# A hand-written order for the experts' stage, weight pieces split whole, and two weight streams for experts with up to 64 tokens

## The chip, the cores and the metric

The kernel runs on one NeuronCore of one Trainium2 chip. The metric is the device time of one execution in microseconds (us), as the median of several executions. The profile is one further execution, recorded by the hardware profiler.

## What is computed

A two-layer decoder trunk on 256 tokens of width 1024, everything in fp32. Each layer runs two groups of attention heads on one input projection, adds their output projection to the residual, and then a feed-forward part: layer 0 a dense SwiGLU of width 2816, layer 1 a router that sends every token to the best two of eight SwiGLU experts of width 3584. The change is about the last part:

```python
def swiglu(h, w_gate, w_up, w_down):
    return (jax.nn.silu(h @ w_gate) * (h @ w_up)) @ w_down

def moe_swiglu(h, router_w, w_gate, w_up, w_down):
    logits = (hf @ router_w).astype(jnp.float32)
    top_logit, top_e = lax.top_k(logits, TOP_K)
    gate = jax.nn.softmax(top_logit, axis=-1)
...
        return swiglu(hf[tok], w_gate[e], w_up[e], w_down[e])
...
    out = jnp.zeros((N, D), jnp.float32).at[row_tok].add(y.reshape(rows, D).astype(jnp.float32) * row_gate[:, None])
```

The router of the reference, on the reference's inputs, gives the eight experts 63, 57, 40, 75, 39, 90, 68 and 80 of the 512 token places. So experts 0, 1, 2 and 4 have at most 64 tokens, the other four have more, and none has over 128.

## The kernel before

**Pieces.** All large weights come from HBM as pieces of 1 MB, [128, 2048] fp32, in the order in which they are used (`Weights.load`, L64 to L73, one DMA each on SP's queue). TensorE multiplies in fp32r, which keeps fewer bits than fp32, so each weight is split into two parts whose sum is exact: ACT copies the piece to fp32r (`whi`, L94), and DVE subtracts that copy from the piece (`wlo`, L95). The data are split in the same way, and a product is three matmul streams (`product3`, L366 to L368): data hi by weight hi, data lo by weight hi, data hi by weight lo. Before, a piece is split in two halves of 1024 columns, and there are five buffers for `whi` and five for `wlo` (N_PART). The pieces themselves lie in four buffers (N_RAW), in the experts' stage also in eight more that attention has left (SPARE), which makes a ring of twelve.

**The experts' stage** (`moe`, from L782). After the router, `gather(e)` puts an expert's tokens into 128 slots: a one-hot matrix `so` picks them out of `h` (32 matmuls `ga`, L830), and ACT and DVE split them (`xe`). The width of 3584 is worked in 7 chunks of 512, so there are 8 x 7 = 56 steps (`seq`). A step uses six pieces: two of gate, two of up, and two of down for the chunk of the step before. Its matmuls, each 128 x 512 in the moving data: 24 `eg` (gate), then 4 `eT` that turn the product of the step before (`turn`, split by ACT into `eth` and by DVE into `etl`), 24 `eu` (up), and 24 `ey` (down). ACT takes Silu of `eg` (`esg`, L906), DVE multiplies with `eu` (`ehc`, L908). At an expert's end `weigh` scales both halves of `ey` with the gates (`yhl`, L304 on ACT, L305 on DVE), and four `scatter` steps (two matmuls and one DVE addition into `acc` each) put the slots back at their tokens, one per step. The next expert is gathered in chunk 3, all at once. `beyond` (behind `tc.If` at L974) would work on slots 128 and up, and is jumped over.

**What sets the order.** The Tile framework's scheduler orders the instructions of each engine from the program and its dependences. Each engine then runs its own list strictly in that order and waits on semaphores.

Of the kernel before, what the change touches and what calls it, by code (L numbers as in the profile page):

```python
# [49 lines left out]
N_RAW, N_PART, SPARE = 4, 5, 8  # L50


class Weights:
    """Weight tiles: loaded in the order of the list, fp32 in, an exact sum of two fp32r parts out."""

    def __init__(self, nc, specs, plain, raw_pool, part_pool, n_raw, n_part):
# [4 lines left out]
        self.spare = {}  # L61
        self.loaded = self.used = 0
# [17 lines left out]
    def take(self):  # L80
# [6 lines left out]
        out = []  # L87
        step = max(1, 1024 // w // 2 * 2)
        for k in range(0, nk, step):
            m = min(step, nk - k)  # L90
            src = raw[:, k:k + m, :].rearrange("p k w -> p (k w)")
            hi = self.part_pool.tile([128, 1024], F32R, name="whi", tag="whi", bufs=self.n_part)
            lo = self.part_pool.tile([128, 1024], F32R, name="wlo", tag="wlo", bufs=self.n_part)
            self.nc.scalar.activation(hi[:, :m * w], src, AF.Copy)  # L94
            self.nc.vector.tensor_tensor(out=lo[:, :m * w], in0=src, in1=hi[:, :m * w].bitcast(F32), op=ALU.subtract)  # L95
            out += [(hi[:, i * w:(i + 1) * w], lo[:, i * w:(i + 1) * w]) for i in range(m)]
        return out
# [3 lines left out]
def trunk_kernel(ctx: ExitStack, tc: tile.TileContext, T: dict, out: bass.AP):  # L101
# [26 lines left out]
    # ---------------------------------------------------------------- weights  # L128
# [52 lines left out]
    # the experts' pieces also go where attention has finished  # L181
# [3 lines left out]
    # -------------------------------------------------------------- constants  # L185
# [64 lines left out]
    # ones, and ones where the row is before the column: exact in bf16  # L250
# [5 lines left out]
    # distance bias, negated, and the mask, as rows over distance + 255  # L256
# [525 lines left out]
    def moe(l, mpool, ht):  # L782
# [137 lines left out]
        def down(e, c, th, tl):  # L920
# [14 lines left out]
            if c == 1:  # L935
                state["place"] = place(e)
# [196 lines left out]
```

## Time and profile before

| | |
|---|---|
| median of 3 runs | 1551.79 us (1550.57 to 1552.54) |
| span of the profiled execution | 1555.6 us (no other time of its own is given; 3.8 us above the median) |
| PE busy | 1527.9 us (98%), 7502 matmuls |
| DVE busy | 1235.4 us (79%) |
| ACT busy | 1026.8 us (66%) |
| POOL busy | 7.8 us (1%) |
| weight pieces of the experts | 336 of 1 MB, 352 of the 434 MB that SP's queue moves |
| experts' stage, first `eg` to the end | 540.8 to 1555.6 us |

PE is TensorE's matmul stream; a matmul's record overlaps the next one's, so the distance between two starts is what a matmul costs. "PEclk" is the granted clock of TensorE as a share of 2.4 GHz. PE has something to do nearly all the time, so the first question at every place is what one step costs on PE, and the second how far behind the next engine is.

### The profile page before, as it was taken

To read this page: it belongs to the slowest core of one execution; us is meant where nothing else is said; L and a number is where in the kernel's file an instruction comes from. 1 tells how busy PE (TensorE), PEld (TensorE's weight loads), DVE (VectorE), ACT (ScalarE), POOL (GpSimd) and SP (SyncE) were. 2 spreads that over 40 slices of the span, in tenths; PEclk is the share of its full clock that TensorE was granted. 3 is DMA by queue.
4 is the path that set the end of the run, shared out by engine and by line. 5 is a ranking of instruction groups with operands and counts; after the bars stand their busy time and mean duration, and the time that the engine had idled before them with its cause. 6 is when DMAs were issued, how large, how long until landed. Compare 5 with 4: busy or idle time off the path is not lost.

```text
span 1555.6 us, 20636 instructions
## 1 busy us (share of the span) xinstructions
PE 1527.9 (98%) x7502; PEld 1234.2 (79%) x7502; DVE 1235.4 (79%) x1771; ACT 1026.8 (66%) x1389; POOL 7.8 (1%) x17
## 2 busy tenths in 40 slices
PE   7999999999999999999999999999999999999997
PEld 6767888888777888888888878887887887887885
DVE  5567755555766798998998888988888889888886
ACT  5445644445545587887787777767777776767774
POOL 2000000000000000000000000000000000000000
PEclk9999999999999999999999999999999999999999
DMA  8812455557626499999999989999999999999980
GB/s 263 292 55 82 157 178 177 200 189 234 229 96 217 167 357 331 379 357 329 361 363 333 363 320 336 344 356 342 326 370 352 327 358 346 329 352 365 353 323 29
DMA packets 200907, 436.94 MB, mean 281 GB/s; under 512 B 9448, under 2 KB 26080, under 8 KB 200800
## 3 DMA queue, kind: packets, MB, share of 16 engines
q1 hardware_dynamic: 198160, 434.63, 79.2%
q8 instruction: 61, 1.00, 0.3%
q10 hardware_dynamic: 2176, 0.52, 0.2%
q0 software_dynamic: 464, 0.40, 0.1%
q14 instruction: 46, 0.38, 0.1%
HBM read 433.92 MB, written 1.08 MB: 280 GB/s over the span
## 4 chain that ended last, share of the span: by engine, by line
PE 95%; DMA 2%; DVE 2%; ACT 1%; issue 1%; SPq 0%; ACTq 0%; DVEq 0%
PE eu L368 7%; PE eg L368 7%; PE eu L367 6%; PE eu L366 6%; PE eg L367 6%; PE eg L366 6%; PE ey L366 6%; PE ey L367 6%; PE ey L368 6%; PE pj L368 3%; PE pj L366 3%; PE pj L367 3%; PE y L368 2%; PE y L367 2%; PE y L366 2%; PE o L502 2%
## 5 line engine op out<-in xcount | busy, mean ns | idle before, releaser
L95 DVE TENSOR_TENSOR wlo<-raw,whi 128x1024 fp32r<-128x1024 f32 (+1 forms) x802 | 946.1, 1215 | 158.9 <-ACT whi L94 147.9
L94 ACT ACTIVATE whi<-raw 128x1024 fp32r<-128x1024 f32 (+1 forms) x802 | 807.0, 1051 | 188.7 <-PE y L367 45.2
L368 PE MATMUL eg<-wlo,xe 128*128 128x512 f32 x448 | 177.4, 396 | 1.5 <-DVE wlo L95 1.5
L368 PE MATMUL eu<-wlo,xe 128*128 128x512 f32 x448 | 178.6, 399 | 0.0
L366 PE MATMUL ey<-whi,eth 128*128 128x512 f32 x448 | 177.5, 397 | 0.7 <-ACT eth L301 0.7
L366 PE MATMUL eg<-whi,xe 128*128 128x512 f32 x448 | 176.8, 395 | 0.7 <-ACT xe L304 0.3
L366 PE MATMUL eu<-whi,xe 128*128 128x512 f32 x448 | 177.4, 396 | 0.0
L367 PE MATMUL ey<-whi,etl 128*128 128x512 f32 x448 | 176.8, 395 | 0.0
L367 PE MATMUL eg<-whi,xe 128*128 128x512 f32 x448 | 175.9, 393 | 0.0
L367 PE MATMUL eu<-whi,xe 128*128 128x512 f32 x448 | 175.2, 391 | 0.0
L368 PE MATMUL ey<-wlo,eth 128*128 128x512 f32 x448 | 165.7, 399 | 0.0
L368 PEld LDWEIGHTS eu<-wlo,xe 128*128 128x128 f32 x448 | 84.1, 188 | 23.9 <-DVE wlo L95 6.9
L368 PEld LDWEIGHTS eg<-wlo,xe 128*128 128x128 f32 x448 | 84.2, 188 | 22.4 <-DVE wlo L95 4.6
L366 PEld LDWEIGHTS ey<-whi,eth 128*128 128x128 f32 x448 | 84.3, 188 | 20.7 <-ACT eth L301 1.1
L367 PEld LDWEIGHTS ey<-whi,etl 128*128 128x128 f32 x448 | 84.5, 189 | 20.2 <-DVE etl L302 0.4
L366 PEld LDWEIGHTS eg<-whi,xe 128*128 128x128 f32 x448 | 84.2, 188 | 20.3 <-ACT whi L94 2.6
L367 PEld LDWEIGHTS eg<-whi,xe 128*128 128x128 f32 x448 | 84.1, 188 | 17.8
L367 PEld LDWEIGHTS eu<-whi,xe 128*128 128x128 f32 x448 | 84.2, 188 | 17.1
L366 PEld LDWEIGHTS eu<-whi,xe 128*128 128x128 f32 x448 | 84.2, 188 | 15.8
L368 PEld LDWEIGHTS ey<-wlo,eth 128*128 128x128 f32 x448 | 82.5, 188 | 17.4
L301 ACT ACTIVATE eth<-eT 128x512 fp32r<-128x512 f32 x56 | 33.1, 592 | 88.7 <-PE ey L368 75.0
L366 PE MATMUL pj<-whi,uhi 128*128 128x512 f32 (+1 forms) x192 | 76.3, 399 | 0.8 <-ACT qv L411 0.8
(299 smaller groups left out, 1970.5 us busy)
## 6 DMA issues: line engine op xcount, KB each, us to landing
raw<-in_exp_w_gate_dram SPq DMA_DIRECT2D x112, 1024.0 KB, 7.0
raw<-in_exp_w_up_dram SPq DMA_DIRECT2D x112, 1024.0 KB, 7.0
raw<-in_exp_w_down_dram SPq DMA_DIRECT2D x112, 1024.0 KB, 6.8
raw<-in_w_in_dram SPq DMA_DIRECT2D x20, 1024.0 KB, 6.0
raw<-in_ffn_w_gate_dram SPq DMA_DIRECT2D x10, 1024.0 KB, 5.1
raw<-in_ffn_w_up_dram SPq DMA_DIRECT2D x10, 1024.0 KB, 5.2
raw<-in_ffn_w_down_dram SPq DMA_DIRECT2D x10, 1024.0 KB, 5.1
raw<-in_cmp_w_dram SPq DMA_DIRECT2D x8, 1024.0 KB, 6.2
```

What stands on the lines that cost most here:

```text
L94: self.nc.scalar.activation(hi[:, :m * w], src, AF.Copy)
L95: self.nc.vector.tensor_tensor(out=lo[:, :m * w], in0=src, in1=hi[:, :m * w].bitcast(F32), op=ALU.subtract)
L301: act.activation(hi, src, AF.Copy)
L366: pe.matmul(dst, xh, wh, start=first, stop=False)
L367: pe.matmul(dst, xl, wh, start=False, stop=False)
L368: pe.matmul(dst, xh, wl, start=False, stop=last)
L502: pe.matmul(o[:, hd * HD:(hd + 1) * HD], pt[:, c:c + 128], vpj[:, j, vc:vc + HD], start=(j == 0), stop=(j == nj - 1))
```

## The change

Four things change.

1. **Split whole.** `split()` makes one ACT and one DVE instruction of 2048 columns per piece; N_PART is three whole pieces (six halves' worth) and N_RAW three, so the ring has eleven pieces in the experts' stage and three elsewhere. This holds for attention and the dense feed-forward too.
2. **Order.** The experts' steps stand under `tc.manual_schedule()`: the program's order is each engine's order. `ahead(1)` splits one piece, three ahead of the one in use, after each product. The next expert's work is spread: slots in chunk 2, half of the gather in chunks 3 and 4, `rl` in chunk 5. `eT` comes at the end of a step.
3. **Two streams.** For an expert with at most 64 tokens (`few`), slots 64 to 127 hold the same tokens again (`own`). POOL copies the hi part of slots 0 to 63 and the lo part of slots 0 to 63 side by side (`mixed`: `xm` per expert, `htm` per step). A matmul with that as its weights gives hi and lo data at once, so up and down need two streams, 16 matmuls a step in place of 24. The sum of the two halves of the slots comes from `both` in the turn, and in the end from the scatter. Gate keeps three streams.
4. **Choice at run time.** The count of the expert is loaded into a register of PE (`value_load`, once per expert), and `by_number` puts an If with both forms around each up piece (2), the turn (1) and each down piece (2): 5 per step, 280 in all. The POOL copies run in both cases.

```diff
-N_RAW, N_PART, SPARE = 4, 5, 8
+N_RAW, N_PART, SPARE = 3, 3, 8
...
+        hi = self.part_pool.tile([128, 2048], F32R, name="whi", tag="whi", bufs=self.n_part)
+        lo = self.part_pool.tile([128, 2048], F32R, name="wlo", tag="wlo", bufs=self.n_part)
+        self.nc.scalar.activation(hi[:, :nk * w], src, AF.Copy)
+        self.nc.vector.tensor_tensor(out=lo[:, :nk * w], in0=src, in1=hi[:, :nk * w].bitcast(F32), op=ALU.subtract)
...
+    def ahead(self, n, loads):
+
+        for _ in range(n):
+            if self.used < len(self.specs):
+                self.ready.append(self.split())
+                self.load(self.used + loads)
...
+        def slots(e):
+
+            own = mpool.tile([128, 128], F32, name="own", tag="own")
+            dve.scalar_tensor_tensor(out=own, in0=again, scalar=few[:, e:e + 1], in1=slot, op0=ALU.mult, op1=ALU.add)
...
+            held[e] += rl, pe.value_load(number[0:1, e:e + 1], min_val=0, max_val=S)
...
+        def by_number(e, many, few):
+
+            with tc.If(held[e][3] > 64) as cond:
+                many()
+            with cond.Else():
+                few()
+
+        def mixed(src, name, n):
+
+            dst = mpool.tile([128, n, 128], F32R, name=name)
+            pool.tensor_copy(dst.rearrange("p k (i t) -> p i k t", i=2), src[:, :, :, 0:64])
+            return dst
...
+            def few():
+                for k, (wh, wl) in enumerate(w, k0):
+                    pe.matmul(b, mix[:, k, :], wh, start=(k == 0), stop=False)
+                    pe.matmul(b, mix[:, k, :], wl, start=False, stop=(k == last))
...
+                for f in range(4):
+                    pe.matmul(b[:, f * 128:(f + 1) * 128], hc[:, f * 128:(f + 1) * 128], both, start=True, stop=True)
...
+        with tc.manual_schedule():
+            prev = None
+            ws.ahead(N_PART, deep)
+            for step in seq + [None]:
+                if step is not None:
+                    e, c = step
+                    _, x, rl, _ = held[e]
+                    if c == 0:
+                        state["xm"] = mixed(x, "xm", KD)
+                    b = mm_bank("eg")
+                    for half in range(2):
+                        product(e, x, b, half * 4, ws.take(), None, KD - 1)
+                        if half:
+                            sg = mpool.tile([128, 512], F32, name="esg", tag="esg")
+                            act.activation(sg, b, AF.Silu, scale=rl)
+                        ws.ahead(1, deep)
+                    b = mm_bank("eu")
+                    for half in range(2):
+                        product(e, x, b, half * 4, ws.take(), state["xm"], KD - 1)
+                        if not half:
+                            ws.ahead(1, deep)
+                    hc = mpool.tile([128, 512], F32, name="ehc", tag="ehc")
+                    dve.scalar_tensor_tensor(out=hc, in0=b, scalar=rl, in1=sg, op0=ALU.mult, op1=ALU.mult)
+                    ws.ahead(1, deep)
+                if prev is not None:
+                    pe_, pc, hts = prev
+                    if pc == 0:
+                        state["y"] = [acc_bank("ey") for _ in range(2)]
+                    down(pe_, pc, 0, ws.take(), hts)
+                    ws.ahead(1, deep)
+                    down(pe_, pc, 2, ws.take(), hts)
+                    if pc == len(MOE_CHUNKS) - 1:
+                        out_of(pe_)
+                if step is not None:
+                    prev = e, c, turn(e, hc)
+                    ws.ahead(1 if (e, c) != seq[0] else 0, deep)
+                    if c == 1:
+                        state["place"] = place(e)
+                    if e + 1 < NE:
+                        if c == 2:
+                            slots(e + 1)
+                        if c in (3, 4):
+                            gather(e + 1, (c - 3) * 4)
+                        if c == 5:
+                            rstd_of(e + 1)
+                for _ in range(1 if step is not None else len(left)):
+                    if left:
+                        scatter(*left.pop(0))
```

Three places of the order, each before and after. First PE at the turn of a step: before, `eT` lies between `eg` and `eu`.

```order
2370 L367 MATMUL eg<-whi,xe 128x512
2371 L368 MATMUL eg<-wlo,xe 128x512
2372 L366 MATMUL eg<-whi,xe 128x512
2373 L367 MATMUL eg<-whi,xe 128x512
2374 L368 MATMUL eg<-wlo,xe 128x512
2375 L914 MATMUL eT<-cc,ehc 128x128 x4
2376 L366 MATMUL eu<-whi,xe 128x512
2377 L367 MATMUL eu<-whi,xe 128x512
2378 L368 MATMUL eu<-wlo,xe 128x512
```

After, at the end of a step, with the two forms of the last down piece and of the turn (L372 to L374 are now the three streams, L989 and L990 the two of `few`):

```order
2326 L374 MATMUL ey<-wlo,eth 128x512
2327 L928 UNCONDITIONAL_BRANCH
2328 L989 MATMUL ey<-whi,htm 128x512
2329 L990 MATMUL ey<-wlo,htm 128x512
2330 L989 MATMUL ey<-whi,htm 128x512
2331 L990 MATMUL ey<-wlo,htm 128x512
2332 L989 MATMUL ey<-whi,htm 128x512
2333 L990 MATMUL ey<-wlo,htm 128x512
2334 L989 MATMUL ey<-whi,htm 128x512
2335 L990 MATMUL ey<-wlo,htm 128x512
2336 L928 UNCONDITIONAL_BRANCH
2337 L928 COMPARE_AND_BRANCH
```

`eT` has moved behind the down product, and of every such block PE runs one of the two forms and jumps over the other.

Second DVE over a step, before (the multiplication `ehc`, the splits, `acc` of a scatter, `etl`):

```order
877 L908 SCALAR_TENSOR_TENSOR ehc<-eu,rl,esg 128x512
878 L95 TENSOR_TENSOR wlo<-raw,whi 128x1024 x4
879 L890 TENSOR_TENSOR acc_4841<-acc_4841,scat 128x512
880 L95 TENSOR_TENSOR wlo<-raw,whi 128x1024 x4
881 L302 TENSOR_TENSOR etl<-eT,eth 128x512
882 L95 TENSOR_TENSOR wlo<-raw,whi 128x1024 x4
883 L908 SCALAR_TENSOR_TENSOR ehc<-eu,rl,esg 128x512
```

And after (L92 is the split, L308 writes the lo half of `eth`):

```order
801 L1027 SCALAR_TENSOR_TENSOR ehc<-eu,rl,esg 128x512
802 L928 UNCONDITIONAL_BRANCH x2
803 L92 TENSOR_TENSOR wlo<-raw,whi 128x2048 x2
804 L308 TENSOR_TENSOR eth<-eT,eth 128x512
805 L92 TENSOR_TENSOR wlo<-raw,whi 128x2048 x2
806 L928 UNCONDITIONAL_BRANCH
807 L92 TENSOR_TENSOR wlo<-raw,whi 128x2048
808 L928 UNCONDITIONAL_BRANCH x2
809 L92 TENSOR_TENSOR wlo<-raw,whi 128x2048
810 L1027 SCALAR_TENSOR_TENSOR ehc<-eu,rl,esg 128x512
```

Twelve halves became six whole splits between two `ehc`, and the five Ifs of a step leave a branch instruction each in DVE's list, as in ACT's, SP's and POOL's.

Third POOL, which had no row between the start and the stage's end, and now has two kinds of copy:

```order
33 L936 COPY htm<-eth 128x2x4x64
34 L936 COPY xm<-xe 128x2x8x64
35 L928 UNCONDITIONAL_BRANCH x5
36 L936 COPY htm<-eth 128x2x4x64
37 L928 UNCONDITIONAL_BRANCH x5
38 L936 COPY htm<-eth 128x2x4x64
```

One copy of 512 elements per partition lies in every step, and one of 1024 at an expert's start.

## Rows read from the trace of the kernel before

**Rows 1.** The page: busy time of the engines.

```profile
PE 1527.9 (98%) x7502; PEld 1234.2 (79%) x7502; DVE 1235.4 (79%) x1771; ACT 1026.8 (66%) x1389; POOL 7.8 (1%) x17
```

**Rows 2.** The chain of waits from 530 us: start, us, what.

```profile
591.13 0.44 PE eT L914 x4
608.11 0.44 PE eT L914 x4
...
707.28 3.57 PE ga L830 x32
...
832.77 3.57 PE ga L830 x32
...
960.30 2.01 PE ga L830 x18
...
1087.67 2.01 PE ga L830 x18
```

**Rows 3.** PE's own instructions in a timeline: start, us, what.

```profile
904.42 0.39 PE L366 MATMUL eg<-whi,xe 128*128 128x512 f32 x1
...
904.65 0.40 PE L367 MATMUL eg<-whi,xe 128*128 128x512 f32 x1
```

**Rows 4.** DVE by form: busy us, mean ns, idle before.

```profile
L95 DVE TENSOR_TENSOR wlo<-raw,whi 128x1024 fp32r<-128x1024 f32 x794 | 940.3, 1220 | 156.8 <-ACT whi L94 145.8 <-PE pj L368 1.1 <-PE pj L367 0.4
L908 DVE SCALAR_TENSOR_TENSOR ehc<-eu,rl,esg 128x512 f32<-128x512 f32 x56 | 41.9, 749 | 18.0 <-PE eu L368 18.0
L302 DVE TENSOR_TENSOR etl<-eT,eth 128x512 fp32r<-128x512 f32 x56 | 38.5, 687 | 10.3 <-ACT eth L301 10.3
L305 DVE SCALAR_TENSOR_TENSOR xe<-ga,gv,xe 128x128 fp32r<-128x128 f32 x64 | 20.6, 346 | 10.4 <-ACT xe L304 10.2
L890 DVE TENSOR_TENSOR acc<-acc,scat 128x512 f32<-128x512 f32 x28 | 19.1, 683 | 4.5 <-PE scat L889 4.4
...
L305 DVE SCALAR_TENSOR_TENSOR yhl<-ey,gs,yhl 128x512 fp32r<-128x512 f32 x16 | 11.5, 746 | 8.4 <-ACT yhl L304 8.4
...
L95 DVE TENSOR_TENSOR wlo<-raw,whi 128x560 fp32r<-128x560 f32 x8 | 5.9, 736 | 2.1 <-ACT whi L94 2.1
```

**Rows 5.** DVE's timeline: splits without a wait between them.

```profile
555.27 3.49 DVE L95 TENSOR_TENSOR wlo<-raw,whi 128x1024 fp32r<-128x1024 f32 x3
```

**Rows 6.** ACT by form.

```profile
L94 ACT ACTIVATE whi<-raw 128x1024 fp32r<-128x1024 f32 x794 | 801.9, 1055 | 180.7 <-PE y L367 43.6 <-PE fu L367 32.7 <-PE eg L367 24.7
...
L94 ACT ACTIVATE whi<-raw 128x560 fp32r<-128x560 f32 x8 | 5.3, 673 | 8.0 <-PE pj L367 6.4 <-PE y L367 1.7
```

**Rows 7.** 20 us windows: PE, PEld, DVE, ACT, POOL, PEclk, DMA share, GB/s.

```profile
640.00:660.00 20.00, 20.00 (x93) 16.43 (x92) 18.38 (x18) 16.12 (x18) 0.00 (x0) 1.00 1.03 387
...
860.00:880.00 20.00, 20.00 (x91) 16.40 (x90) 18.22 (x18) 16.02 (x17) 0.00 (x0) 1.00 1.02 365
920.00:940.00 20.00, 19.60 (x85) 14.74 (x84) 18.30 (x19) 14.76 (x17) 0.00 (x0) 1.00 0.91 336
```

**Rows 8.** The page: DMA issues, us to landing.

```profile
raw<-in_cmp_w_dram SPq DMA_DIRECT2D x8, 1024.0 KB, 6.2
```

**Rows 9.** The If over `beyond` and its flag: min/median/max ns.

```profile
L974 PEldq COMPARE_BRANCH  x1: 4622/4622/4622, 1548.2 to 1548.2; - x1
L974 DVEq COMPARE_BRANCH  x1: 72/72/72, 1549.0 to 1549.0; - x1
...
L876 PEldq TENSOR_LOAD <-flag x1: 484/484/484, 1547.6 to 1547.6; - x1
```

**Rows 10.** PE's sequencer at a wait, and weight loads during it.

```profile
L559 PEldq EVENT_SEMAPHORE  x2: 1432/2636/3839, 48.7 to 396.3; - x2
...
400.45 0.59 PEld L559 LDWEIGHTS hid<-raw,xp 128*32 128x32 f32 x24 [0.35 <-issue]
```

**Rows 11.** 4 us windows around PE's pauses, columns as in group 7.

```profile
48.00:52.00 4.00, 2.31 (x12) 1.42 (x12) 4.00 (x22) 1.29 (x3) 0.00 (x0) 1.00 1.10 348
52.00:56.00 4.00, 4.00 (x41) 2.48 (x42) 3.86 (x17) 0.00 (x0) 0.00 (x0) 0.57 0.78 217
```

More of the change, by code (lines that the diff above doesn't have):

```diff
@@ L61, in __init__ @@
         self.spare = {}
+        self.ready = []
         self.loaded = self.used = 0
@@ L816, in moe @@
                                  op0=ALU.add, op1=ALU.mult)
+        cb = tr_bank("count")
+        for t in range(NT):
+            pe.matmul(cb[:, 0:NE], ones, sel[:, t, :], start=(t == 0), stop=(t == NT - 1))
+        few = mpool.tile([128, NE], F32, name="few")
+        dve.tensor_scalar(out=few, in0=cb[:, 0:NE], scalar1=64.0, scalar2=None, op0=ALU.is_le)
+        number = mpool.tile([128, NE], I32, name="number")
+        dve.tensor_copy(number, cb[:, 0:NE])
+        most = mpool.tile([128, 1], F32, name="most")
@@ new lines, in gather, with rstd_of @@
+        def gather(e, k):
+            so, x = held[e][:2]
+            b = tr_bank("ga")
+            for j in range(4):
+                for t in range(NT):
+                    pe.matmul(b[:, j * 128:(j + 1) * 128], h[t][:, (k + j) * 128:(k + j + 1) * 128], so[:, t, :],
+                              start=(t == 0), stop=(t == NT - 1))
+            for j in range(4):
+                split_psum(x[:, 0, k + j, :], x[:, 1, k + j, :], b[:, j * 128:(j + 1) * 128], gain(R_FN, l, k + j))
+        def rstd_of(e):
+            so = held[e][0]
@@ L867, in place @@
             return st, gs
-        cb = tr_bank("count")
-        for t in range(NT):
-            pe.matmul(cb[:, 0:NE], ones, sel[:, t, :], start=(t == 0), stop=(t == NT - 1))
-        most = mpool.tile([128, 1], F32, name="most")
-        dve.tensor_reduce(out=most, in_=cb[:, 0:NE], axis=AX.X, op=ALU.max)
         flag = mpool.tile([128, 1], I32, name="flag")
@@ L944, in moe @@
-        prev = None
-        left = []
-        parts_of = []
-        def between():
-            if prev is not None:
-                parts_of[:] = turn(prev[2])
-        for i, (e, c) in enumerate(seq):
-            if c == 3 and e + 1 < NE:
-                gather(e + 1)
-            hc = gate_up(e, c, between)
-            if prev is not None:
-                down(*prev[:2], *parts_of)
-            for _ in range(PER if c else 0):
-                if left:
-                    scatter(*left.pop(0))
-            prev = (e, c, hc)
@@ L962, in moe @@
-        between()
-        down(*prev[:2], *parts_of)
-        for e, n, t, st, yhl in left:
-            scatter(e, n, t, st, yhl)
+        def by_number(e, many, few):
[7 more added lines that the diff above has]
+            return dst
@@ new lines, in down, with steps, many, few @@
+        def down(e, c, k0, w, hts):
+            ht, htm = hts
+            y = state["y"]
+            ends = c == len(MOE_CHUNKS) - 1
+            def steps():
+                for i, (wh, wl) in enumerate(w):
+                    for n in range(2):
+                        f = slice(n * 512, (n + 1) * 512)
+                        yield y[n], k0 + i, wh[:, f], wl[:, f]
+            def many():
+                for o, k, wh, wl in steps():
+                    product3(o, ht[:, 0, k, :], ht[:, 1, k, :], wh, wl, c == 0 and k == 0, ends and k == 3)
+            def few():
+                for o, k, wh, wl in steps():
+                    pe.matmul(o, htm[:, k, :], wh, start=(c == 0 and k == 0), stop=False)
+                    pe.matmul(o, htm[:, k, :], wl, start=False, stop=(ends and k == 3))
+            by_number(e, many, few)
```

114 lines of the change are left out of this document (44 added, 70 removed).

## Prediction

> **What bounds the kernel now.** I read the busy times first: PE has work for 98% of the span, DVE for 79%, ACT for 66%, POOL for nothing [rows 1]. Then the chain of waits, for the period of a step: two turns of quiet steps start 16.98 us apart [rows 2], and matmuls start 0.23 us apart [rows 3], so 72 of them and the turn are the step, and PE's own work is what a step costs. From the gather of one expert to the next it is 125.5 us, later 127.5 and 127.4 [rows 2]; in the windows PE is full (20.00 of 20) except once per expert at its end, where it shows 19.60 and the period is 1.9 us longer [rows 7]: ACT holds the next splits behind `yhl`, which waits for the last `ey`. DVE has 16 to 18 us of work in such a 20 us window and the DMA engines a share of 0.91 to 1.03 [rows 7]. So the reader is to see a stage that PE sets, with two other resources close behind. A cut of PE's work gains only as far as the next one.
>
> **The two streams.** A few-step has 16 matmuls less: on PE 16.98 - 16 x 0.23 = 13.3 us. DVE keeps all of its work, so I add that up. A split of 2048 columns isn't in the trace. Columns cost (1220 - 736) / 464 = 1.043 ns each [rows 4]; three splits in a run take 3.49 us [rows 5], so one follows the other by (3.49 - 1.22) / 2 = 1.135, and 1024 more columns add 1.07: 2.20 us per whole split in a run. Bounds are 2.20 and 2.29 (one alone, 1.22 + 1.07); I take the run, since DVE now works without a pause. Per expert: 42 x 2.20 = 92.4, `ehc` 7 x 0.749 = 5.2, `etl` 7 x 0.687 = 4.8, `xe` 8 x 0.346 = 2.8, `acc` 4 x 0.683 = 2.7, `yhl` 2 x 0.746 = 1.5 [rows 4], and some 1.2 for slots, `rl` and gates (small ones, each under an `xe`). That is 110.6 us, or 15.8 a step: **DVE becomes the bound of the few-steps**, and 2.5 of the 3.7 us that PE gives up are lost to it. To it come waits within DVE's fixed list. Before, `ehc` waited 18.0, `etl` 10.3 and `xe` 10.4 us over eight experts [rows 4], together 4.8 per expert; the hand order puts two splits ahead of each, so I take 3 (bounds 0 and 4.8).
>
> **The POOL copies.** They are new, and nothing in the trace shows POOL and DVE at work together. By the nearest row of that size a copy of 512 columns is 0.69 us (`etl`). PE needs `htm` only after the next step's 24 gate and 16 up matmuls (9 us) and `xm` after 24 (5.5 us), so PE doesn't wait. What the copy costs DVE lies between nothing and its whole 0.69 us in each of 7 steps, 4.8 per expert; I take half, 2.4, as nothing shows which end is nearer. The Trainium skill has a rule that speaks against this part: "SBUF — State Buffer", section "Who interferes with whom", says that a DVE instruction with two SBUF inputs, as the split is, and a GpSimd instruction that reads SBUF exclude each other for the whole instruction. No row here can test it; by it the upper end holds, and that is a rival below.
>
> A few-expert is then 110.6 + 3 + 2.4 = 116.0 us. Experts 0, 1 and 2 took 125.5 each and expert 4 took 127.4: **gain 3 x 9.5 + 11.4 = 39.9 us.**
>
> **The four other experts.** PE's work stays. The hand order removes the hold at the expert's end (1.9 us), but a scatter now stands in PE's list where `yhl` is barely ready (about 1 us), and one where the bank of `etl` is (about 1 us). I take 0, bounds -1.9 and +2 per expert. Three whole parts are enough: a split takes ACT 1.055 + 1024 x (1055 - 673) / 464 = 1.90 us [rows 6] and DVE 2.29, 4.2 in a row and some 0.2 of signals, against 5.5 for the two pieces that PE works on meanwhile.
>
> **The Ifs.** 280 on PE, half of them with a taken jump over 12 pairs of instructions, half over 8. A compare and branch takes 72 ns on DVE and 4622 on PE, for one jump over all of `beyond` [rows 9]. The trace has no short jump on PE. Its sequencer runs ahead: it was held 3.84 us at a wait, and the weight loads behind it paused for 0.35 us only [rows 10], so what it loses at one If is covered by queued work unless it is over 3 us; in the few-steps another 3 us a step of slack come on top. I take nothing for PE (the other end is the slower rival). The load of the count is one per expert, 0.48 us [rows 9], covered likewise. On DVE five branch instructions a step could cost up to 5 x 0.072 us in the 28 few-steps, 10 us; they have nothing to compare, and I take 1.
>
> **DMA.** A few-step still needs six pieces, 6.29 MB, now in 16.6 us: 380 GB/s. The queue showed 387 at a share of 1.03 in its best window and 365 at 1.02 [rows 7], so at 365 it brings 5.78 pieces a step, and the ring drains by 0.22 a step, or 5 pieces over the 21 few-steps of experts 0 to 2; of eleven about eight are ahead. Expert 3 fills it again. I take no cost; if the lead goes, DMA is late next.
>
> **Start, end, attention.** At the start of the stage fewer pieces are loaded ahead (eleven buffers, not twelve), the first split is a whole piece (+1.9), and the router has some ten small instructions more while the gather keeps PE busy: 2 us. At the end the last splits are whole pieces: 1.5. In both attention layers three raw buffers instead of four make a fourth compression piece wait for the first one's matmuls, at most once a layer for the 6.2 us of a transfer [rows 8]: bounds 0 and 12.4; projections are there to fill in, so 3.
>
> **Sum.** -39.9 + 1 + 2 + 1.5 + 3 = -32.4. The profiled execution spans 1555.6 us, 3.8 above the median of the runs: 1555.6 - 32.4 = 1523.2, and as a median **1519.4, some 1520 us.**
>
> **Rivals.**
>
> 1. *DMA sets the few-steps.* For it: shares of 1.02 at 365 GB/s leave no reserve, and a ring that frees a buffer only after `wlo` asks late. Against it: 387 in one window, and the lead. At 350 GB/s, 5.54 pieces a step, the ring loses 0.46 x 21 = 9.7, and the steps after that cost 18 us: some 6 us. At the 336 of the third window it loses 14, six pieces too many at 3.1 us, 19 us; with expert 4, up to 25. So 1526 to 1545. Chance 0.12.
> 2. *POOL's copies shut DVE out.* Upper end of that term: 2.4 us more in each of four experts, an `xm` of twice the size each (1.4), and POOL waiting in turn for a split: 15 to 25 us more, 1535 to 1545. For it only that both engines read SBUF; against it, DVE has some idle time in each step into which the copy fits. Chance 0.09.
> 3. *Slower: the Ifs are not covered.* If PE's sequencer cannot feed matmuls over a branch, each If in the four large experts, where PE is the bound, costs its own time: 140 of them, so from 32.4 / 140 = 0.23 us each the gain is gone; at 0.5 us the time is 1590, and toward the 4.62 us of the row it would be far beyond. For it: that row. Against it: that jump passes several hundred instructions, these 16 or 24, DVE's over 27 rows of its list took 72 ns, and the queue of rows 10. The Trainium skill, "Runtime: NRT & Kernel Launch", section "Instruction fetch mechanics", has it that only a taken jump out of the fetched window stalls; by it short jumps are mostly free and the row of 4.62 us is such a stall, which agrees with the two rows but is shown by no short jump on PE here. Chance 0.11.
> 4. *Slower: the clock.* PE at 2.31 of 4 us was followed by a window at 0.57, the granted clock having fallen from 2.4 to 1.2 GHz for a part of it [rows 11]. Few-steps keep PE at 13.3 of 16.6, 3.2 of 4, in pauses of half a microsecond. Were they to run at the lower level, 56 matmuls would take 26 us, 28 x 9.4 = 260 us more. Chance 0.03.
> 5. *No change.* Attention at its upper bound (+9), branches on DVE (+9), the four large experts (+8) and a part of rival 2 eat the gain together: 1549 to 1555. Chance 0.05.
>
> **How the numbers follow.** The forecast has 0.60: 1505 to 1535. Its best case has DVE without waits and copies (110.6): 3 x 14.9 + 16.8 = 61.5 us of gain, less 3.5 at start and end, 1494. The range goes from there through rivals 1 and 2 to the lower half of 5, 1550, and leaves out rivals 3 and 4, and some of 5. A difference under 0.2% (3.1 us) can't be told from none. Faster by more: 0.60 + 0.12 + 0.09 = 0.81. Same: 0.05. Slower: 0.11 + 0.03 = 0.14.
>
> **What would show it.** Right: in the windows of the first three experts DVE at 18.5 of 20 or more with PE near 16.5; steps of 16.6 us there and 18.1 for the others; splits of 2.2 to 2.3 us; `eg` waiting for `wlo`. Rival 1: DVE idle for raw pieces. Rival 2: splits that begin with a copy's end, or last longer beside one. Rival 3: PE idle behind L928 in the large experts. The prediction is wrong if few-steps fall to PE's 13.4 us, or if the large experts lose more than 2 us each.

## The result, and the profile after

The changed kernel takes 1590.1 us (median of 4 runs, 1581.9 to 1600.4) against 1552.2: the ratio is 1.025, with an interval of 1.021 to 1.029. It is slower by 38 us where 32 us of gain were forecast. The profiled execution spans 1588.4 us, 32.8 more than before. Where the executions of one kernel lie more than 1.5% apart, ratios here are taken from the faster ones.

PE's work did fall, as the page of the changed kernel says (compare [rows 1]), but the span grew, so PE now has idle time:

```profile
PE 1480.0 (93%) x7166; PEld 1188.0 (75%) x7166; DVE 1203.2 (76%) x1387; ACT 985.0 (62%) x991; POOL 112.3 (7%) x81
```

**Where the 32.8 us lie.** The last product of the router (`lg`) starts at 526.3 us before and at 545.0 after (its last start stands behind "to"):

```profile
L789 PE MATMUL lg<-wg,ht x32: 174/256/277, 521.5 to 526.3; 128*128 128x8 f32 x32
L795 PE MATMUL lg<-wg,ht x32: 174/256/380, 539.4 to 545.0; 128*128 128x8 f32 x32
```

So 18.7 us are lost ahead of the experts. The stage begins with the first `eg`, at 534.6 us before (the table of the kernel before has 540.8, which is too late) and at 554.5 after. From the first `eg` of an expert to that of the next (for expert 7, to its last `ey`) I count, before and after: the few-experts 0, 1, 2 and 4 take 118.9, 125.5, 125.5 and 127.3, and 118.6, 128.0, 129.4 and 125.3, together 4.1 us more; the large ones 3, 5, 6 and 7 take 127.8, 127.4, 127.4 and 130.1, and 130.8, 130.8, 129.3 and 130.2, together 8.4 more; the start of the stage and its end cost 1.5. That is the whole difference.

The windows show what kind of loss it is. Experts 1 (few) and 3 (large) before, columns as in [rows 7] (start and end, then the length and the busy time of each engine):

```profile
653.40:778.90 125.50, 125.50 (x583) 103.55 (x582) 115.57 (x117) 99.21 (x110) 0.00 (x0) 1.00 0.97 352
904.40:1032.20 127.80, 127.40 (x587) 103.13 (x586) 112.42 (x116) 90.81 (x107) 0.00 (x0) 1.00 0.95 342
```

The same experts after, with expert 2 between them:

```profile
673.10:801.10 128.00, 112.13 (x501) 88.49 (x500) 110.85 (x76) 90.43 (x67) 19.32 (x8) 0.96 0.96 347
801.10:930.50 129.40, 113.51 (x501) 89.29 (x500) 110.87 (x76) 90.36 (x67) 19.32 (x8) 0.95 0.95 341
930.50:1061.30 130.80, 125.71 (x577) 103.01 (x576) 112.57 (x77) 91.34 (x67) 11.34 (x8) 0.99 0.94 341
```

In a few-expert DVE has 110.85 us of work, which is the 110.6 of the prediction. But the expert takes 128: neither PE (112) nor DVE is full, and the DMA engines, at a share of 0.96, bring 347 GB/s, less than the 352 of expert 1 before. The time is in waits that pass from engine to engine. The clock is below 1.00 in these windows too.

**One such wait, followed.** The first step of expert 2, from the timeline of all engines after the change (start, us, engine; in brackets the idle time before, and what ended it):

```profile
804.22 2.61 POOL L936 CAST htm<-eth 128x512 fp32r<-128x512 f32 x1 [15.89 <-DVE eth L308]
...
806.78 3.09 POOL L936 CAST xm<-xe 128x1024 fp32r<-128x1024 f32 x1
...
809.93 0.80 PE L947 MATMUL eu<-whi,xm 128*128 128x512 f32 x1 [3.11 <-POOL xm L936]
...
813.32 1.91 ACT L91 ACTIVATE whi<-raw 128x2048 fp32r<-128x2048 f32 x1 [3.98 <-PE eu L947]
...
815.26 2.29 DVE L92 TENSOR_TENSOR wlo<-raw,whi 128x2048 fp32r<-128x2048 f32 x1 [3.25 <-ACT whi L91]
...
823.69 0.51 PE L920 MATMUL scat<-yhl,st 128*128 128x512 f32 x1 [2.17 <-DVE yhl L311]
```

POOL's copies take 2.61 and 3.09 us beside DVE's splits, PE waits 3.11 us for `xm`, ACT waits 3.98 for PE to free a part, DVE 3.25 for ACT, and at the step's end PE waits again, 2.17 us in the scatter, for `yhl`. (A part is one of the buffers for `whi` or `wlo`.) The windows of 4 us over the first part:

```profile
804.00:808.00 4.00, 2.81 (x13) 2.00 (x11) 4.00 (x3) 2.97 (x3) 3.78 (x2) 1.00 0.99 378
808.00:812.00 4.00, 2.07 (x5) 1.69 (x6) 3.60 (x2) 1.34 (x1) 1.87 (x1) 0.66 1.04 392
812.00:816.00 4.00, 4.00 (x11) 3.11 (x10) 0.75 (x2) 1.91 (x1) 0.00 (x0) 0.50 1.05 388
```

After PE's pause the granted clock is 0.66 and 0.50 of full speed, 1.2 GHz for some 7 us, as after the pause in [rows 11]; PE shows 4.00 of 4 there, but its matmuls start 0.43 us apart in place of 0.23. So the step takes 22.9 us, and the one without extra work at the expert's end 15.4.

The waits of that expert (engine, what waited for what, us in total, times, longest):

```profile
...
DVE wlo L92 <- ACT whi L91: 14.5, 11, 4.0
ACT whi L91 <- PE eg L373: 9.0, 4, 5.0
...
ACT whi L91 <- PE eu L947: 5.7, 3, 4.0
ACT esg L1019 <- PE eg L374: 5.2, 5, 1.1
...
PEld scat L919 <- DVE eth L308: 3.7, 2, 2.4
```

These are the questions for the runs: the Ifs, the copies, the places of `esg` and of the scatters in the lists, the chain PE, ACT, DVE, PE through three parts, and what delays the layers ahead.

### The profile page after: what moved, and what is told of

Read it like the earlier page. It is cut to its first block, busy times and chain, and to the rows that moved or that the text cites. A ratio compares the mean times of both kernels' runs of the same rounds, so it can differ in the third digit from the quotient of the medians.

```text
span 1588.4 us, 19387 instructions
## 1 busy us (share of the span) xinstructions
PE 1480.0 (93%) x7166; PEld 1188.0 (75%) x7166; DVE 1203.2 (76%) x1387; ACT 985.0 (62%) x991; POOL 112.3 (7%) x81
## 4 chain that ended last, share of the span: by engine, by line
PE 66%; DVE 15%; DMA 6%; ACT 6%; issue 5%; POOL 1%; SPq 0%; ACTq 0%; DVEq 0%
DVE wlo L92 12%; ACT whi L91 5%; PE eg L372 4%; PE eg L373 4%; PE eg L374 4%; DMA raw<-in_exp_w_gate_dram 4%; PE pj L372 3%; PE ey L373 3%; PE ey L372 3%; PE eu L374 3%; PE pj L374 3%; PE pj L373 2%; PE ey L374 2%; PE eu L372 2%; PE eu L373 2%
## 5 line engine op out<-in xcount | busy, mean ns | idle before, releaser
L92 DVE TENSOR_TENSOR wlo<-raw,whi 128x2048 fp32r<-128x2048 f32 x404 | 910.6, 2275 | 226.8 <-ACT whi L91 218.4
L91 ACT ACTIVATE whi<-raw 128x2048 fp32r<-128x2048 f32 x404 | 758.8, 1892 | 241.0 <-PE eg L373 57.8
L372 PE MATMUL eg<-whi,xe 128*128 128x512 f32 x448 | 181.1, 404 | 0.0
L374 PE MATMUL eg<-wlo,xe 128*128 128x512 f32 x448 | 178.0, 397 | 0.0
L936 POOL CAST htm<-eth 128x512 fp32r<-128x512 f32 x56 | 88.3, 1577 | 909.9 <-DVE eth L308 909.9
L990 PE MATMUL ey<-wlo,htm 128*128 128x512 f32 x224 | 95.3, 425 | 15.6 <-DVE wlo L92 13.6
L948 PE MATMUL eu<-wlo,xm 128*128 128x512 f32 x224 | 93.2, 416 | 13.7 <-DVE wlo L92 13.7
L374 PEld LDWEIGHTS eg<-wlo,xe 128*128 128x128 f32 x448 | 86.2, 192 | 19.1
L372 PEld LDWEIGHTS eg<-whi,xe 128*128 128x128 f32 x448 | 86.7, 193 | 17.7
L947 PE MATMUL eu<-whi,xm 128*128 128x512 f32 x224 | 91.7, 409 | 6.7 <-POOL xm L936 6.2
L374 PE MATMUL eu<-wlo,xe 128*128 128x512 f32 x224 | 87.9, 392 | 3.7 <-DVE wlo L92 3.7
L989 PE MATMUL ey<-whi,htm 128*128 128x512 f32 x224 | 91.2, 407 | 0.0
L372 PE MATMUL ey<-whi,eth 128*128 128x512 f32 x224 | 87.8, 392 | 0.7 <-ACT eth L307 0.7
L374 PE MATMUL ey<-wlo,eth 128*128 128x512 f32 x224 | 87.5, 391 | 0.5 <-DVE wlo L92 0.5
L372 PE MATMUL eu<-whi,xe 128*128 128x512 f32 x224 | 87.2, 389 | 0.0
L373 PE MATMUL eu<-whi,xe 128*128 128x512 f32 x224 | 87.2, 389 | 0.0
L372 PE MATMUL pj<-whi,uhi 128*128 128x512 f32 (+1 forms) x192 | 77.2, 402 | 1.1 <-ACT qv L417 1.1
```

What stands on the lines that cost most here:

```text
L91: self.nc.scalar.activation(hi[:, :nk * w], src, AF.Copy)
L92: self.nc.vector.tensor_tensor(out=lo[:, :nk * w], in0=src, in1=hi[:, :nk * w].bitcast(F32), op=ALU.subtract)
L372: pe.matmul(dst, xh, wh, start=first, stop=False)
L373: pe.matmul(dst, xl, wh, start=False, stop=False)
L374: pe.matmul(dst, xh, wl, start=False, stop=last)
L936: pool.tensor_copy(dst.rearrange("p k (i t) -> p i k t", i=2), src[:, :, :, 0:64])
```

## The experiments

All runs were compared with the kernel before, measured again on the same chip each time. The profile of a run is split in two, since these parts move apart: the start of the router's last product ("ahead"), and the time from there to the end of the span ("rest"). Before: 526.3 and 1029.3. After: 545.0 and 1043.4.

**e1_static: no Ifs.** The choice is made when the program is built, from the known counts.

```diff
+FEW = (0, 1, 2, 4)
...
-            with tc.If(held[e][3] > 64) as cond:
+            if e in FEW:
+                few()
+            else:
                 many()
-            with cond.Else():
-                few()
```

> The changed kernel with the choice between three and two streams made when the program is built (experts 0, 1, 2 and 4 get two streams): no If, no register load, all else as it was, POOL copies included. If the Ifs cost what was lost (rival 3 of the prediction), the steps of the few-experts fall by over 1 us and the time falls by 30 us or more, to 1560 or less. If the loss lies in waits of the fixed order, with Ifs that are covered, the time stays within 1580 to 1592.

Measured 1588.6 us (1583.1 to 1594.1); rest 1044.2, the changed kernel's 1043.4. The Ifs cost nothing that can be seen, and rival 3 falls. The changed kernel's own row of branches on PE's sequencer (min/median/max ns):

```profile
L928 PEldq COMPARE_BRANCH  x420: 65/169/417, 558.0 to 1573.1; - x140
```

**e2_three: the hand order and the whole splits.** Three streams for all experts, no POOL copies, no Ifs. The buffers are those of the changed kernel.

```diff
+FEW = ()
...
-            return ht, mixed(ht, "htm", 4)
+            return ht, None
```

> The hand order and whole splits alone: three streams for every expert, no Ifs, no POOL copies. If the hand order loses by itself, every expert takes 129 to 131 us, as the large ones of the changed kernel, and the time is 1585 to 1595, so that two streams were worth nothing. If the two streams with their POOL copies are what costs, experts take 126 to 127.5 us and the time is 1565 to 1575 (what is left over 1552 lies ahead of the experts' stage).

Measured 1602.9 us (1598.5 to 1607.4). Experts take 129.5 us from expert 1 on (expert 0 123.2), so the hand order with these buffers loses 2 to 4 us per expert without two streams, copies or Ifs. The first theory had these times for the experts, but put them down to the order alone; this run doesn't separate the order from the buffers (e11_before_whole below has the buffers without the order). The time is above that theory's range, because ahead is 553.8 in this execution; rest is 1051.4. The window of expert 1:

```profile
686.10:815.60 129.50, 126.23 (x586) 103.49 (x583) 110.59 (x76) 91.61 (x67) 0.00 (x0) 1.00 0.94 341
```

With the same buffers and order, two streams were worth 8 us of the rest (1051.4 to 1043.4), not 40.

**e3_xm: `xm` earlier.** The copy for the next expert stands behind the last up product of the one before.

```diff
+                    if c == len(MOE_CHUNKS) - 1 and e + 1 < NE:
+                        mixes[e + 1] = mixed(held[e + 1][1], "xm", KD)
                     hc = mpool.tile([128, 512], F32, name="ehc", tag="ehc")
```

> The changed kernel with one move: POOL's copy xm for the next expert is issued behind the last up product of the expert before, ahead of that step's htm, not at the new expert's start. If the late xm (3.1 us of waiting in TensorE, and the half clock after it) makes the first step of a few-expert long, that step falls from 22 to 23 us to about 18, and the time by 3 x 4 to 3 x 5 us (experts 1, 2 and 4), to about 1576. If the long first step comes from the scatters and yhl, nothing changes: 1585 to 1592.

Measured 1576.6 us in the profiled execution; the other one, at a lower clock, took 1612.0. The first step does fall, from 21.7, 22.9 and 18.9 us to 18.9, 19.1 and 18.9, but the second then takes 20.6 and 21.6 in experts 1 and 2 (19.0 before the move), and the last 16.2 (15.4). Rest is 1040.0: 3.4 us gained where 12 to 15 were expected. That 1576.6 is the time that was expected is luck: the other 10.2 us come from ahead (534.8, not 545.0). A miss: the wait moved on to the next place in the list.

**e6_before_raw3: the kernel before with three raw pieces.**

```diff
-N_RAW, N_PART, SPARE = 4, 5, 8
+N_RAW, N_PART, SPARE = 3, 5, 8
```

> The kernel before with three raw buffers for four (a ring of eleven for twelve) and nothing else. If the missing raw buffer is what made the layers ahead of the experts 19 us longer in the changed kernel, the router starts about 15 us later and the time is 1565 to 1572. If that loss comes from whole splits or fewer parts, the time stays at 1552 to 1556.

Measured 1562.5 us (median of 8, 1557.0 to 1566.4), ratio 1.006 (1.004 to 1.008). The profiled execution is the fastest of these (1557.0) and shows no delay ahead (525.6), so it doesn't say where the other runs lose 1 to 9 us more. Between the two expectations: three raw pieces cost some of it, not 19 us.

**e5_halves: splits in halves, order as in the changed kernel.**

```diff
-N_RAW, N_PART, SPARE = 3, 3, 8
+N_RAW, N_PART, SPARE = 3, 6, 8
...
-        hi = self.part_pool.tile([128, 2048], F32R, name="whi", tag="whi", bufs=self.n_part)
...
+            hi = self.part_pool.tile([128, 1024], F32R, name="whi", tag="whi", bufs=self.n_part)
```

> The changed kernel with each piece split as before, in halves of 1024 columns, six half buffers of each part in place of three whole ones; order, Ifs and copies as they were. If the chain through three whole parts (TensorE ends a piece, ACT 1.9 us, DVE 2.2 us, TensorE again) is what keeps DVE at 111 of 128 us in a few-expert, the few-experts fall to 117 to 120 us and the attention layers lose about 10 us less: 1540 to 1555. If the waits come from what stands in the lists between the splits (yhl, gather, esg, scatters), the few-experts stay at 125 to 128 and only the layers ahead gain: 1573 to 1583.

Measured 1563.3 us (1562.1 to 1568.5); ahead 539.3, rest 1022.2. Neither theory alone: a step without extra work falls from 15.4 to 14.9 and expert 0, which has no scatters, from 118.6 to 111.8, so the chain through the parts was real. But experts 1 and 2 stay at 126.8, with first steps of 24.5 and 24.4 us. Of the rest, 21.2 us are gained with the order as it was.

**e4_order: three moves in the lists, whole pieces.** `xm` as in e3_xm, Silu behind the next split on ACT, the scatter behind the gate product.

```diff
                         product(e, x, b, half * 4, ws.take(), None, KD - 1)
+                        if half and left:
+                            scatter(*left.pop(0))
+                        ws.ahead(1, deep)
                         if half:
                             sg = mpool.tile([128, 512], F32, name="esg", tag="esg")
                             act.activation(sg, b, AF.Silu, scale=rl)
-                        ws.ahead(1, deep)
```

> The changed kernel, whole pieces, with three moves in the lists: xm copied behind the last up product of the expert before, Silu (esg) on ACT behind the next split in place of ahead of it, and the scatter behind the gate product in place of behind the turn, so that TensorE doesn't wait for yhl and the lo part of eth. If places in the lists are what costs, a large expert falls from 130 to about 127 us and a few-expert from 128 to 120 or less: 1540 to 1560. If the chain through three parts is the limit, the few-experts stay over 124 and the time over 1570.

Measured 1524.7 to 1550.4 us over 8 runs. The granted clock differs between these runs (0.971 to 0.991), so they scatter more than those of other kernels; the ratio is 0.990 (0.985 to 0.995), from the three of them that took 1524.7, 1540.3 and 1542.6. The profiled execution took 1549.2, at a clock of 0.972: rest is 992.4, 51 us less than in the changed kernel, and ahead 554.9, the worst but one. In the experts' windows the clock is at 1.00, so these can be compared. Few-experts (1) and large ones (3):

```profile
681.90:798.60 116.70, 108.27 (x501) 84.42 (x500) 110.94 (x76) 90.44 (x67) 21.71 (x8) 1.00 1.01 376
915.30:1040.30 125.00, 123.74 (x577) 101.72 (x576) 111.98 (x77) 91.22 (x67) 12.68 (x8) 1.00 0.97 359
```

DVE is now at 110.94 of 116.70 and the few-expert within 1 us of the 116.0 of the prediction. Its waits for `whi`, 13.0 us in expert 1 of the changed kernel, are down to

```profile
DVE wlo L92 <- ACT whi L91: 1.5, 1, 1.5
```

What the two streams were to bring is there, once PE, ACT and DVE no longer wait at these three places.

**e9_xm_scat: without the move of Silu.**

```diff
-                        ws.ahead(1, deep)
                         if half:
                             sg = mpool.tile([128, 512], F32, name="esg", tag="esg")
                             act.activation(sg, b, AF.Silu, scale=rl)
+                        ws.ahead(1, deep)
```

> The run with the three moves (e4_order) without the move of Silu on ACT: xm early and the scatter behind the gate product. If the scatters in TensorE's list carry the gain, few-experts stay near 117 us and large ones at 125 to 127. If Silu ahead of the next split carries it, few-experts are at 122 or more.

Measured 1549.0 us (1534.6 to 1560.0); few-experts 118.7 to 119.6 us, large ones 125.3 to 127.5; rest 1002.4. With e3_xm's 1040.0 and e4_order's 992.4: `xm` is worth some 3 us, then the scatter's place some 38, then Silu's some 10. These prices hold for moves made in this order and with whole parts; the scatter wasn't moved alone.

**e7_all: halves and the three moves.**

> Halves and the three moves together. If both causes are real and add up, few-experts come near DVE's 111 to 115 us, large ones to 126 to 127, the layers ahead near those of before: 1505 to 1525. If DVE and POOL are kept apart by something else, few-experts stay over 120 us and the time over 1540.

Measured 1534.2 us (1533.6 to 1534.8), ratio 0.989 (0.986 to 0.992); ahead 541.6, rest 991.2. Not the 1505 to 1525 expected: few-experts take 110.5 to 119.2, but the layers ahead stay late, and halves add nothing to the three moves in the rest (992.4 in e4_order). With halves the three moves are worth 31 us of the rest (e5_halves to this run), with whole parts 51 (the changed kernel to e4_order): the order and the parts are not two separate prices.

**e8_sched: two streams in the scheduler's order.** Halves, no hand order, no Ifs, `htm` copied for the few-experts only.

```diff
-        with tc.manual_schedule():
+        if True:
```

> Halves, two streams for experts 0, 1, 2 and 4 fixed when the program is built, POOL copies htm only for these, no Ifs, and the order of the experts' stage by the framework's scheduler as in the kernel before (no hand order). If the hand order is what gave the gain away, few-experts take 112 to 116 us and large ones 126 to 127: 1500 to 1520. If two streams cannot gain for another reason (POOL, the clock, DMA), few-experts stay over 120 us in any order: 1530 or more.

Measured 1564.3 us; ahead 541.3, rest 1021.1, experts 2 and 4 take 127.7 and 125.9. By its numbers that is the second expectation, but its "in any order" doesn't hold: with the same halves e7_all has 119.2 and 115.5. The scheduler's order doesn't find the gain either: there PE's weight load waits 6.4 us for `htm` in expert 1, and POOL's copies wait in turn for `ey` to free their buffer. So the gain is a matter of the order, but not of a hand order as such.

**e10_best: the three moves with the buffers of the kernel before** (four raw pieces, five halves of each part, two pieces split ahead).

```diff
-N_RAW, N_PART, SPARE = 3, 6, 8
+N_RAW, N_PART, SPARE = 4, 5, 8
```

> The three moves, with the buffers of the kernel before: four raw pieces, five halves of each part, splits two pieces ahead. If the buffers are what made the layers ahead of the experts late, the router's last product ends at 526 to 530 us again, and with few-experts at 116 to 120 the time is 1505 to 1522, faster than both kernels. If those layers are late for another reason, it ends at 537 or later and the time is 1525 to 1540.

Measured 1539.5 us (1535.9 to 1543.2), ratio 0.991. Ahead is 526.9: the buffers are the cause there. But rest is 1014.5, 23 more than in e7_all, few-experts at 122 (expert 0 at 115.5) and large ones at 127 to 129.5, and the 1505 to 1522 expected are missed: five halves, with splits only two pieces ahead, are too few for the experts' stage.

**e11_before_whole: the kernel before with the changed kernel's buffers.**

```diff
-N_RAW, N_PART, SPARE = 4, 5, 8
+N_RAW, N_PART, SPARE = 3, 3, 8
...
-        step = max(1, 1024 // w // 2 * 2)
+        step = nk
```

> The kernel before with the changed kernel's buffers alone: whole splits, three raw pieces, three whole parts, order by the scheduler, three streams. If whole splits with these buffers make the layers ahead late, the router's last product ends at 537 to 550 us (526 before, 526 with three raw pieces and halves) and the time is 1563 to 1580. If they don't, it ends by 530.

Measured 1617.5 us; ahead 555.1, in the kernel before's own order. That settles the place: the 18.7 us ahead of the experts come from the buffers, not from the experts' code. The rest is worse too (1060.6 against 1029.3, and against the 1051.4 of e2_three): with three whole parts the scheduler's order loses more than the hand order does.

**e12_raw4_whole: four raw pieces, three whole hi parts, two whole lo parts**, with the three moves.

```diff
-        lo = self.part_pool.tile([128, 2048], F32R, name="wlo", tag="wlo", bufs=self.n_part)
+        lo = self.part_pool.tile([128, 2048], F32R, name="wlo", tag="wlo", bufs=self.n_part - 1)
...
-            ws.ahead(N_PART, deep)
+            ws.ahead(2, deep)
```

> The three moves with whole splits, but four raw pieces, three whole hi parts and two whole lo parts, splits two pieces ahead. If the fourth raw piece is what the layers ahead lack, the router's last product ends at 526 to 531 us. If two lo parts are enough in the experts' stage, few-experts take 117 to 121 us and large ones 125 to 128: 1510 to 1525, faster than both kernels. If whole splits make the layers ahead late even with four raw pieces, that product ends at 537 or later and the time is 1528 or more.

Measured 1687.4 us, ratio 1.085, where 1510 to 1525 were expected for two lo parts being enough; few-experts take 138 to 139 (expert 0 128), large ones 144; ahead 547.8. The window of expert 1:

```profile
684.50:822.90 138.40, 114.72 (x502) 86.67 (x500) 111.04 (x75) 89.54 (x67) 5.67 (x8) 0.96 0.90 319
```

Same work as in e4_order, 21.7 us more: one lo part less, split one piece less ahead, costs more than all else in this study. And the layers ahead are late even with four raw pieces, if the parts are whole and the lo parts two.

**e13_parts6: memory by stage.** Ahead of the experts the buffers of the kernel before; in the stage three raw pieces and six halves, the sixth in the place of the fourth raw piece; the three moves.

```diff
+            if self.halves and self.halves % 6 == 0:
+                both = self.part_pool.tile([128, 2048], F32R, name="w6", tag="r3")
+                hi, lo = both[:, 0:1024], both[:, 1024:2048]
...
+    ws.spare.update({i: "r3" for i in range(3, first, 4)})
```

> The run e7_all (halves and three moves) with the memory shared out by stage: ahead of the experts four raw pieces and five halves as in the kernel before, in the experts' stage three raw pieces and six halves (the fourth raw piece's place serves as the sixth half of both parts). If the buffers ahead of the experts' stage cause the late start, the router's last product ends at 526 to 529 us in place of 542, experts take as long as in e7_all (110 to 119 and 125 to 127), and the time is 1515 to 1523. If something else in the changed kernel delays those layers, it ends at 536 or later and the time is 1530 to 1537.

Measured 1516.6 us (1516.1 to 1520.5), ratio 0.977 (0.975 to 0.979): faster than both kernels. Ahead 519.4, rest 994.8; experts as in e7_all. The loss ahead and the loss in the experts' stage are repaired apart, and the repairs add up.

**e14_act_xm: and `xm` on ACT.**

```diff
+                        act.activation(mixes[e + 1].rearrange("p k (i t) -> p i k t", i=2),
+                                       held[e + 1][1][:, :, :, 0:64].bitcast(F32), AF.Copy)
```

> The run e13_parts6 with the copy xm on ACT in place of POOL (128 x 1024, seven per execution). If POOL's copies, kept out by DVE's splits, are what makes the first step of a few-expert 19.9 us in e7_all, that step falls to 15 to 17 us, a few-expert to 115 to 117, and the time is 3 to 9 us under e13_parts6. If not, both are within 3 us.

Measured 1514.9 us (1512.4 to 1517.7), ratio 0.975 (0.973 to 0.976), so 1.7 us under e13_parts6 by the medians, within the spread of both. (Ahead is 524.9 here and 519.4 there, though nothing ahead differs, so single profiles tell it only within some 5 us.) The first steps of experts 1 and 2 stay at 20.9 and 21.0 us. It isn't `xm` that makes them long: PE waits 4.0 us there for `htm`, which is still on POOL.

**The layers ahead, in windows.** Before the change, layer 1's attention (columns as in [rows 7]):

```profile
440.00:460.00 20.00, 20.00 (x113) 14.75 (x111) 11.80 (x39) 11.43 (x29) 0.00 (x0) 1.00 0.17 57
460.00:480.00 20.00, 18.88 (x97) 14.68 (x96) 16.98 (x48) 10.00 (x18) 0.00 (x0) 1.00 0.87 311
```

After:

```profile
440.00:460.00 20.00, 19.25 (x77) 12.61 (x77) 11.19 (x49) 6.74 (x24) 0.00 (x0) 0.77 0.22 83
460.00:480.00 20.00, 20.00 (x94) 16.16 (x94) 9.36 (x19) 6.99 (x13) 0.00 (x0) 0.72 0.16 53
480.00:500.00 20.00, 16.49 (x69) 12.51 (x69) 15.39 (x47) 9.14 (x15) 0.00 (x0) 0.88 0.45 152
```

And in e13_parts6:

```profile
440.00:460.00 20.00, 20.00 (x118) 15.60 (x118) 12.39 (x34) 9.34 (x21) 0.00 (x0) 1.00 0.32 107
460.00:480.00 20.00, 18.83 (x101) 14.07 (x100) 15.79 (x58) 12.08 (x25) 0.00 (x0) 1.00 0.31 105
```

With the changed buffers PE isn't full at first (19.25 of 20, where it was 20.00), and the clock is at 0.77 and 0.72 where it stays at 1.00 with the old ones. That this gap is what lowered it isn't shown: before, PE shows 18.88 of 20 at a clock of 1.00. The compression's last matmul (`hid`) starts at 420.2 us in place of 407.6. Not every execution falls as deep: ahead was 534.8 to 555.1 in the profiles of kernels with whole parts. The changed kernel's runs spread over 18 us, those of e13_parts6 over 4.

## Why the prediction was wrong

- **Where the miss lies.** Between a gain of 32.4 us and a loss of 32.8 in the span are 65 us: 44.0 in the few-experts (a gain of 39.9 forecast, a loss of 4.1 measured), 8.4 in the large ones, 15.7 ahead; start, end and Ifs took about 3 less than forecast. A small part is a misreading: expert 0 took 118.9 us before, not 125.5, as its first step has no down product.
- **DVE's sum** came out right, 110.6 us forecast and 110.85 measured, but in part by luck: the splits take 95.66 us of expert 1, not 92.4 (one is 2.30 us in the stage's mean, near the upper bound of 2.29 and not the 2.20 of a run), and the rest of DVE's list 3 us less than its terms.
- **The failed step** is the term "waits within DVE's fixed list ... I take 3 (bounds 0 and 4.8)". It measured 17 us in expert 1 (128.0 - 110.85), 16 to 19 in the four. I added up the waits of `ehc`, `etl` and `xe`, and left out the first line of [rows 4]: the splits' own wait for ACT's copy, 156.8 us over the kernel before. DVE's waits in expert 1 after the change:

```profile
DVE wlo L92 <- ACT whi L91: 13.0, 10, 4.0
DVE xe L311 <- ACT xe L310: 2.6, 6, 0.4
DVE wlo L92 <- PE eu L948: 1.4, 1, 1.4
```

  What I had added up came to 2.6, near my 3; what I had left out came to 14.4. In the new lists a wait in one engine passes to the others: PE at a scatter frees no part, so ACT can't split, so DVE idles. I had named this wait ("a scatter now stands in PE's list where `yhl` is barely ready"), priced it at 1 us, and charged it to the large experts only. e3_xm and e9_xm_scat show that the scatter's place is worth some 38 us of the rest once `xm` is moved. The waits need the few parts too: e5_halves gains 21.2 us with the order unchanged.
- **"Three whole parts are enough"** compared 4.2 us of a split with 5.5 of two large pieces. In a few-step two up or down pieces are only 2 x 8 x 0.23 = 3.7 us, and Silu or a turn stands between the splits on ACT. e5_halves (expert 0 at 111.8) and e12_raw4_whole (138) show how much hangs on it.
- **The large experts** lost 3.0, 3.4, 1.9 and 0.1 us, near or over my upper end of 2; e2_three shows 129.5 without any copy or If, so neither is the cause. The order and the three whole parts are it together: moves in the order alone bring them to 125.0 (e4_order), and the parts alone make the scheduler's order slower still (e11_before_whole). No run has three streams, halves and the unmoved order.
- **Attention**: 3 us forecast with bounds 0 and 12.4, 18.7 measured. My bound priced the raw pieces and left out the parts and the clock. e11_before_whole reproduces it (28.8), e13_parts6 undoes it. How much each of the two buffers does is settled in part. The compression of layer 1, from its first `hid` to its last, takes 7.2 us with four raw pieces and halves (before, e10_best, e13_parts6, e14_act_xm), 16.8 or 16.9 in the profiles with three, whole parts or halves, and 13.9 with four and whole parts (e12_raw4_whole): a raw piece less holds it up by 9.7 us, where I had 6.2. Whether that is lost goes with the clock. In e6_before_raw3, e1_static and e3_xm, where the windows from 440 to 500 stay at 0.91 or more, PE makes most of it good: 61.6 or 61.7 us from the last `hid` to the last projection, against 69.2 before. In the changed kernel, at 0.77 and 0.72, it is 70.7. Why the clock falls in one execution and not in another stays open; ahead is 525.6 with three raw pieces and five halves, 539 to 542 with six halves (e5_halves, e7_all, e8_sched).
- **The POOL copies** cost DVE little: its split lasts 2.306 us in experts 1 and 2, and 2.288 in those of e2_three, which has no copies. That is 0.8 us per expert of 42 splits, where I took 2.4. They cost POOL, and through a late `xm` or `htm` PE. I had the right rule and the wrong loser. One copy beside splits and one without, in expert 3:

```profile
950.70 2.61 POOL L936 CAST htm<-eth 128x512 fp32r<-128x512 f32 x1 [11.39 <-DVE eth L308]
969.79 0.61 POOL L936 CAST htm<-eth 128x512 fp32r<-128x512 f32 x1 [16.48 <-DVE eth L308]
```

  The Trainium skill ("SBUF — State Buffer", section "Who interferes with whom") has the two kinds of instruction exclude each other; the trace agrees, 2.61 against 0.61 us, the difference being most of one split.
- **The rivals**: rival 3 gave the sign and the very size by a wrong cause; e1_static rules it out. What the Trainium skill says ("Runtime: NRT & Kernel Launch", section "Instruction fetch mechanics"), that a taken jump stalls where its target isn't fetched yet, fits the 0.17 us that a branch takes here in the median. Rival 4 was half right: the clock does fall in the few-experts, to its half for some 10 of 128 us (2 x 0.04 x 128), but behind the waits: in e4_order, with the same matmuls, it stays at 1.00. Rival 1 had no part in it: DVE waits 1.2 us for a raw piece in expert 2 and not at all in expert 1, and e4_order draws 376 GB/s at 116.7 us. No rival of mine had the mechanism that decided, a fixed order, over few parts, in which waits are passed round.

## What to carry to other kernels

When an order is written by hand, take every instruction that waits for another engine (here Silu, the scatter, a turn) and ask what stands behind it in the list: put a split or a product whose inputs are ready ahead of it. The sum of the busiest engine's work is a floor, which is reached only if no engine's wait holds another's buffers; count the buffers for the shortest product, not the longest. And a pool that serves several stages is sized by each of them: the experts' stage wanted six halves, attention a fourth raw piece, and giving each its own, together with the three moves, turned 38 us of loss into 37 of gain.

## What was not expected of the hardware

- A copy on POOL beside an unbroken run of splits on DVE can be kept out for long. In e13_parts6, with splits of 1024 columns, the copy of 0.62 us took 9.49: DVE ran eight splits meanwhile, and the copy ended at 654.76, during DVE's next instruction of another kind (`ehc`, 654.20 to 654.95, which reads `eu` from PSUM):

```profile
645.27 9.49 POOL L950 CAST htm<-eth 128x512 fp32r<-128x512 f32 x1 [8.08 <-DVE eth L322]
663.38 0.62 POOL L950 CAST htm<-eth 128x512 fp32r<-128x512 f32 x1 [8.62 <-DVE eth L322]
```

- The 420 branches of the 280 Ifs, whose jumps pass 8 or 12 pairs of matmuls, take PE's sequencer 0.17 us in the median and at most 0.42, and no time is lost that e1_static could show; the 4.62 us of [rows 9] are no measure for a short jump.
